# Attention and retention values computed token by token in a hybrid block: whole 512-column products, with the last 16 tokens on their own

## The chip, the cores and the metric

The kernel runs on one core of one Trainium2 chip. The metric is the device time of one execution in microseconds. A core has TensorE (PE, whose weight loads are shown as PEld), VectorE (DVE), ScalarE (ACT), GpSimd (POOL) and the DMA queues of SyncE (SP), ACT and POOL. PE reads its operands from the on-chip memory SBUF and writes to PSUM, eight banks of 512 float32 columns by 128 partitions; DVE and ACT bring results from PSUM back to SBUF.

## The reference

One transformer layer on 512 tokens with 16 meta tokens ahead of them (528 rows, width 1024): a SwiGLU block at half weight, a mixer, a second SwiGLU block, a final norm. The mixer is where the change lies:

```python
proj = u @ w_in                      # u = rmsnorm(h), 528 x 1024
rq, rk, rv, rg, aq, ak, av, iq, ik, iw, g_ret, g_att = split(proj)
# retention: 4 heads, keys of 256, values of 512
y = ((q @ k.T) * decay) @ v          # in chunks, with a carried state
yr = (silu(rg) * rmsnorm(y)) @ w_ret_out
# attention: 8 heads of 128; an index score picks 128 keys for a query
score = sum_h iw_h * relu(iq_h @ ik.T)
ya = softmax(q @ k_selected.T) @ v_selected @ w_att_out
merged = sigmoid(g_ret) * yr + sigmoid(g_att) * ya
h = h + merged @ w_mix_out
```

Both `rv` (4 x 512 columns) and `av` (8 x 128 columns) are products of the same 528 normalized rows with columns of `w_in`.

## The kernel before, in words

Activations lie feature by feature: a tile has 128 features in its partitions and the 528 tokens along its columns. Each float32 operand is split into a high part (an ACT copy rounded to the format fp32r) and a low part (a DVE subtraction of the high part), and a product is three matmuls: high by high, low by high, high by low (`mm3`, L145 to L153, whose matmuls stand at L152). Weights come in by `load_w` (L130, SP's queue) into one of two buffers `raw` of 1 MB, and `split_w` (L136) makes `whi` and `wlo`, three buffers each, by the helper `split` (L116; ACT at L117, DVE at L118). `Cols` (L155) hands out one block of 128 columns after another. The normalization is not applied to the activations themselves: their products are multiplied by R, one over the root mean square of each token, which `rstd_steps` makes (L200).

PE's order is the program's own order, since the kernel schedules PE by hand; on the other engines a scheduler orders instructions by their place in the program and their dependences. While the mixer runs, PSUM has two tiles of two banks (`mm_tile`) and four of one bank (`sm_tile`).

The mixer's stages, in PE's order, are these. First come the index queries (psiq, L573) and the index keys (psik, L588), with rotary tables that POOL multiplies by R (`rope_tables`, L525). Then follow four retention heads (L803 to L877). Each head has two query blocks (psrq), two key blocks (psrk), the output product of the head before (`ret_out`, psro, L701), then four times a gate block (`gated`, psrg, L846) and a value block (`values`, psrv, L854), and once the decayed scores (`decayed`, psst, L745). Steps of a background generator stand between them: index scores (pssc, L606) in head 0, and from head 1's output on the top-k search on DVE (L629).

A value block is 128 value features by 528 tokens, in two halves of 264 columns. The weighted sum needs the tokens in the partitions. So `values` multiplies the block by R on DVE (L857), `by_token` (L788) transposes it on PE in four blocks of 128 tokens and one of 16 (psvt, L791 and L792), and ACT and DVE split the result. The last 16 tokens go into a small stacked tile of 80 rows (`vtail`, by `split_rows`, L654), which is multiplied by an equally stacked tile of scores in one matmul (L775). `weigh` (L777) makes the weighted sum pspv (L774), the squares for the norm, and the gated output.

Attention (L884 to L992) does the same for each of eight heads: query, key and value blocks (psaq, psak, psav; the value at L919), scores (psS, L927), transposed probabilities (psPT, L950), weighted sum (psao, L966), and the transposes of the next value block. Four blocks of the retention's output gates are done behind head 7's scores and the last two after it (L983 to L989, L1000); then come eight gate blocks for attention (psga, L1004), the attention output product (psat), and the mixing product (psmo).

The change replaces `values`, `by_token` and `proj_v` (L919) by one new function, and touches `tails` (L650), `weighted` (L768), `weigh`, `rstd_of` (L210), the index stage (L568 to L603) and both head loops. The first SwiGLU block's last loop (L512 to L519) gets one small POOL instruction per feature block. The second SwiGLU block's output product already has tokens in the stationary operand and 512 features in the moving one (psd, L1146); it is not touched.

Of the kernel before, what the change touches and what calls it, by code (L numbers as in the profile page):

```python
# [18 lines left out]
P = 128  # L19
D = 1024  # L20
# [61 lines left out]
def kernel(ctx: ExitStack, tc: tile.TileContext, x, meta, g1, wg1, wu1, wd1, gm,  # L82
# [117 lines left out]
    def rstd_steps(ssum, n, dim, dst, sp, psum):  # L200


        ends = [min(b * P, n - P) for b in range(-(-n // P))]
        nb = len(ends)
        col = psum()
        for b, t0 in enumerate(ends):
            nc.tensor.matmul(col[:, b : b + 1], ssum[:, t0 : t0 + P], ones, start=True, stop=True)
        yield from rstd_of(col, n, dim, dst, sp, psum, P - (n - S))

    def rstd_of(col, n, dim, dst, sp, psum, tail):  # L210
# [4 lines left out]
        r = sp.tile([P, 5], F32, tag="rcol", name="rcol", bufs=2)  # L215
# [34 lines left out]
    hd = dpool.tile([KD, P, S], F32, name="hd")  # L250

# [4 lines left out]
    gap(cpool, 8)  # L256


    with pool("f1") as fp, pool("gps", 2, PSUM) as gps, ExitStack() as later:
# [205 lines left out]
        for f0, nf in ((0, 12), (12, 10)):  # L465
# [38 lines left out]
            for c in range(0, KD, 2):  # L504
# [61 lines left out]


    with pool("ixt") as ixt:  # L568
# [11 lines left out]
        cos, sin = rope_tables(0, ixt)  # L580
        iq = []
        for i in range(4):
# [4 lines left out]
            iq.append((h, l))  # L587
        w = Cols(w_in, OFF_IK, 1).next()  # L588
# [61 lines left out]
    def tails(p, n):  # L650

        tp.update(v=[stacked(p, f"vtail{i}", P) for i in range(2)], p=stacked(p, "ptail", n), turn=0)
# [27 lines left out]
    with pool("rt") as rt:  # L680
        tp.update(pool=rt, bufs=7)
        cos, sin = rope_tables(2, rt)
        gap(rt, 48)
# [41 lines left out]
        def proj_real(cols, name):  # L725
            w = cols.next()
            ps = sm_tile(name)
            mm3([(ps, REAL)], w, xs, KD)
            return ps

        def proj_all(cols, name):
            w = cols.next()
            parts, ps = halves(mm_tile(name))
            mm3(parts, w, xs, KD)
            return ps

# [31 lines left out]
        def weighted(ps, vb, prob):  # L768

            for kb in range(4):  # L770
                vh, vl = vb[0][:, kb, :], vb[1][:, kb, :]
# [3 lines left out]
            nc.tensor.matmul(ps[:, KQ[4] :], vb[2][:TR], tp["p"][:TR, :NM], start=False, stop=True)  # L775

        def weigh(c, vb, sg, prob, ssum, o):  # L777
# [5 lines left out]
            oh = rt.tile([P, S], F32R, tag=f"oh{c}", name="oh")  # L783
            ol = rt.tile([P, S], F32R, tag=f"ol{c}", name="ol")
            split(t[:, :S], oh, ol)
            o.append((oh, ol))

        def by_token(vt, vp):  # L788
            ps = mm_tile("psvt").rearrange("p (a b) -> p a b", a=2)
            for kb in range(4):  # L790
                nc.tensor.transpose(ps[:, 0, kb * P : (kb + 1) * P], vt[:, kb * P : (kb + 1) * P], ident)  # L791
            nc.tensor.transpose(ps[:NM, 1, 0:P], vt[:, 4 * P : T], ident)  # L792
            vh = vp.tile([P, 4, P], F32R, tag="vh", name="vh", bufs=2)
            vl = vp.tile([P, 4, P], F32R, tag="vl", name="vl", bufs=2)
            split(ps[:, 0, :].rearrange("p (b c) -> p b c", b=4), vh, vl)
            tail = tp["v"][tp["turn"]]
            tp["turn"] ^= 1
            split_rows(ps[:NM, 1, 0:P], tail, "hhl")
            return vh, vl, tail
# [3 lines left out]
        for h in range(RH + 1):  # L803
            if h == RH:
# [4 lines left out]
                break  # L809
            u = rt.tile([P, UW], F32, tag="u", name="u")  # L810
            nc.scalar.dma_start(u, decay[h])
            cols = Cols(w_in, OFF_RQ + h * DK, 2)
            if h == 0:
                steps, bg[0] = bg[0], iter(())
# [9 lines left out]
            cols = Cols(w_in, OFF_RK + h * DK, 2)  # L824
            if h == 0:
                bg[0] = steps
            ka = proj_all(cols, "psrk")
            next(norm, None)
            step()
            kb_ = proj_all(cols, "psrk")  # L830
            next(norm, None)
            rk = rope_pair(ka, kb_, cos, sin, T, "rk")
            step()
# [8 lines left out]
            cv = Cols(w_in, OFF_RV + h * DV, 4)  # L842
# [11 lines left out]
            def values():  # L854
                ps = proj_all(cv, "psrv")
                vt = tmp()
                ins = nc.vector.tensor_tensor(vt, ps, R, ALU.mult)  # L857
                step(ins)
                return vt

            for c in range(4):
                if c == 0:
                    sg = gated()
                    vt = values()
                    prob = decayed(rq, rk, u)
                else:
                    vt = values()
                    sg = gated()
                    weigh(*pend, prob, ssum, o)
# [3 lines left out]
                pend = (c, by_token(vt, rt), sg)  # L873
# [9 lines left out]

    with pool("ao") as ao:  # L884
        ao_parts = []
        with pool("at") as at:
# [11 lines left out]
            cq, ck, cv = (Cols(w_in, o_, AH, step=1) for o_ in (OFF_AQ, OFF_AK, OFF_AV))  # L898
# [20 lines left out]
            def proj_v():  # L919
                w = cv.next()  # L920
                parts, ps = halves(mm_tile("psav"))
                mm3(parts, w, xs, KD)
                vt = tmp()
                nc.vector.tensor_tensor(vt, ps, R, ALU.mult)
                return vt

            def scores(q, k):  # L927
                for j in (3, 2, 1, 0):
# [37 lines left out]
            def weigh_v(parts, v):  # L966
                ps = sm_tile("psao")
                weighted(ps, v, parts)
                oh = ao.tile([P, S], F32R, tag=f"ah{len(ao_parts)}", name="ah")
                ol = ao.tile([P, S], F32R, tag=f"al{len(ao_parts)}", name="al")  # L970
                split(ps, oh, ol)
                ao_parts.append((oh, ol))

            q, k, vt = proj_q(), proj_k(), proj_v()
            for h in range(AH):
                more = h + 1 < AH
                scores(q, k)
                if h == 0:
# [12 lines left out]
                if more:  # L991
                    v = by_token(vt, at)  # L992
# [5 lines left out]
        with pool("ou") as ou:  # L998
            tp.update(pool=ou, bufs=3)
            for c in (6, 7):  # L1000
                gate_acc(c, gate(gr, ou))
            cols = Cols(w_in, OFF_GA, KD)
            sa = []
            for c in range(KD):  # L1004
                w = cols.next()
                ps = sm_tile("psga")
                mm3([(ps, REAL)], w, xs, KD)
                t = ou.tile([P, S], F32, tag=f"sa{c}", name="sa")
                nc.vector.tensor_tensor(t, ps, Rr, ALU.mult)
                nc.scalar.activation(t, t, AF.Sigmoid)  # L1010
                sa.append(t)
# [54 lines left out]
    mgs.close()  # L1066
    accs.close()
# [117 lines left out]
```

## Time and profile before

| | |
|---|---|
| median of 3 runs | 1591.05 us (1590.24 to 1592.95) |
| the profiled execution's own time | 1590.52 us |
| span from its first to its last instruction | 1588.7 us |
| mean granted TensorE clock | 0.999 |
| values in retention / attention (psrv / psav) | 256 / 128 matmuls of each of three kinds |
| value transposes (psvt) | 96 of 128 tokens, 24 of 16 |
| mean memory traffic | 94 GB/s |

In the profile a row of the grouped view gives the source line, the engine, the operation, the output tile and its inputs by the program's names with their shapes, the number of instructions, their busy time and the mean of one in ns, and the idle time of the engine ahead of them with the instruction that ended most of it. Matmuls overlap: the time listed for one is longer than the distance to the next. The chain of waits follows the work back from the last instruction; its pieces are start, length, and what ran. A piece "PE psrv L152 x48" is 48 matmuls in a row without a wait. The table of stages gives, for each stretch, its length, the busy time of PE, PEld, DVE, ACT and POOL, the granted clock, the DMA share and the rate. A wait row gives the line that waited, what it waited for, the total, the number and the longest.

### The profile page before, as it was taken

To read this page: it belongs to the slowest core of one execution; us is meant where nothing else is said; L and a number is where in the kernel's file an instruction comes from. 1 tells how busy PE (TensorE), PEld (TensorE's weight loads), DVE (VectorE), ACT (ScalarE), POOL (GpSimd) and SP (SyncE) were. 2 spreads that over 40 slices of the span, in tenths; PEclk is the share of its full clock that TensorE was granted. 3 is DMA by queue.
4 is the path that set the end of the run, shared out by engine and by line. 5 is a ranking of instruction groups with operands and counts; after the bars stand their busy time and mean duration, and the time that the engine had idled before them with its cause. 6 is when DMAs were issued, how large, how long until landed. Compare 5 with 4: busy or idle time off the path is not lost.

```text
span 1588.7 us, 23011 instructions
## 1 busy us (share of the span) xinstructions
PE 1576.4 (99%) x9731; PEld 1419.7 (89%) x9731; DVE 820.0 (52%) x1263; ACT 569.3 (36%) x912; POOL 230.9 (15%) x187
## 2 busy tenths in 40 slices
PE   9999999999999999999999999999999999999998
PEld 8999999999888898899898999988888888888886
DVE  5443234334575776866845766753454444334434
ACT  6322222223544333233333555552234332223223
POOL 1211001111310201302204110011002111001100
PEclk9999999999999999999999999999999999999999
DMA  5222232224422231231313322322233332232222
GB/s 192 83 89 78 97 109 80 97 80 141 134 88 67 67 116 54 80 117 40 120 54 92 95 67 67 93 72 88 91 128 108 111 105 81 94 113 86 93 92 81
DMA packets 148582, 148.66 MB, mean 94 GB/s; under 512 B 3288, under 2 KB 137456, under 8 KB 148480
## 3 DMA queue, kind: packets, MB, share of 16 engines
q1 hardware_dynamic: 143872, 138.16, 27.0%
q10 hardware_dynamic: 4544, 9.03, 1.7%
q8 instruction: 76, 1.25, 0.3%
q14 instruction: 26, 0.21, 0.0%
q0 software_dynamic: 64, 0.01, 0.0%
HBM read 143.00 MB, written 4.19 MB: 93 GB/s over the span
## 4 chain that ended last, share of the span: by engine, by line
PE 94%; DVE 3%; ACT 1%; issue 1%; POOL 1%; DMA 0%; ACTq 0%; POOLq 0%; DVEq 0%
PE psu L152 16%; PE psg L152 15%; PE psd L152 8%; PE psd L1146 7%; PE psrv L152 6%; PE psrg L152 6%; PE psrk L152 3%; PE psak L152 3%; PE psav L152 3%; PE psrq L152 3%; PE psgate L152 3%; PE psro L152 3%; PE psmo L152 3%; PE psaq L152 3%; PE psat L152 3%; PE psga L152 3%
## 5 line engine op out<-in xcount | busy, mean ns | idle before, releaser
L117 ACT ACTIVATE whi<-raw 128x1024 fp32r<-128x1024 f32 (+3 forms) x284 | 278.0, 981 | 840.1 <-PE psu L152 165.5
L118 DVE TENSOR_TENSOR wlo<-raw,whi 128x1024 fp32r<-128x1024 f32 (+3 forms) x284 | 339.7, 1196 | 177.2 <-ACT whi L117 173.6
L152 PE MATMUL psu<-xl,whi 128*128 128x264 f32 (+1 forms) x528 | 141.0, 319 | 0.0
L152 PE MATMUL psu<-xh,whi 128*128 128x264 f32 (+1 forms) x528 | 140.6, 318 | 0.0
L152 PE MATMUL psu<-xh,wlo 128*128 128x264 f32 (+1 forms) x528 | 140.5, 318 | 0.0
L152 PE MATMUL psg<-xl,whi 128*128 128x264 f32 (+1 forms) x496 | 133.3, 321 | 0.0
L152 PE MATMUL psg<-xh,whi 128*128 128x264 f32 (+1 forms) x496 | 132.8, 320 | 0.0
L152 PE MATMUL psg<-xh,wlo 128*128 128x264 f32 (+1 forms) x496 | 132.8, 321 | 0.0
L152 PEld LDWEIGHTS psu<-xh,wlo 128*128 128x128 f32 x528 | 88.1, 188 | 6.8
L152 PEld LDWEIGHTS psu<-xh,whi 128*128 128x128 f32 x528 | 87.8, 188 | 6.9
L152 PEld LDWEIGHTS psu<-xl,whi 128*128 128x128 f32 x528 | 87.5, 188 | 6.9
L152 PEld LDWEIGHTS psg<-xh,wlo 128*128 128x128 f32 x496 | 82.6, 188 | 6.8
L152 PEld LDWEIGHTS psg<-xh,whi 128*128 128x128 f32 x496 | 82.3, 188 | 6.8
L152 PEld LDWEIGHTS psg<-xl,whi 128*128 128x128 f32 x496 | 82.0, 188 | 6.8
L486 POOL TENSOR_TENSOR t<-t,R 128x528 f32<-128x528 f32 x22 | 37.6, 1711 | 262.3 <-ACT t L485 262.3
L1121 POOL TENSOR_TENSOR t<-t,R 128x512 f32<-128x512 f32 x22 | 38.5, 1751 | 251.6 <-ACT t L1120 251.6
L152 PE MATMUL psd<-hl,whi 128*128 128x264 f32 x352 | 71.3, 284 | 0.0
L152 PE MATMUL psd<-hh,wlo 128*128 128x264 f32 x352 | 70.8, 283 | 0.0
L152 PE MATMUL psd<-hh,whi 128*128 128x264 f32 x352 | 70.6, 282 | 0.0
L1146 PE MATMUL psd<-whi,hh 128*128 128x512 f32 x176 | 68.5, 389 | 0.0
L1146 PE MATMUL psd<-wlo,hh 128*128 128x512 f32 x176 | 68.5, 389 | 0.0
L1146 PE MATMUL psd<-whi,hl 128*128 128x512 f32 x176 | 68.5, 389 | 0.0
(316 smaller groups left out, 3543.1 us busy)
## 6 DMA issues: line engine op xcount, KB each, us to landing
raw<-in_w_in_dram SPq DMA_DIRECT2D x34, 1024.0 KB, 4.9
raw<-in_ffn_w_up_dram SPq DMA_DIRECT2D x22, 1024.0 KB, 5.0
raw<-in_ffn_w_gate_dram SPq DMA_DIRECT2D x21, 1024.0 KB, 5.0
raw<-in_w_in_dram SPq DMA_DIRECT2D x25, 512.0 KB, 3.4
raw<-in_ffn_w_down_dram SPq DMA_DIRECT2D x10, 1024.0 KB, 4.8
raw<-in_w_ret_out_dram SPq DMA_DIRECT2D x16, 512.0 KB, 3.4
raw<-in_ffn_w_down_dram SPq DMA_DIRECT2D x8, 768.0 KB, 4.3
raw<-in_ffn_w_down_dram SPq DMA_DIRECT2D x8, 640.0 KB, 3.9
```

The costliest lines, as they stand in the source:

```text
L117: nc.scalar.activation(hi, src, AF.Copy)
L118: eng.tensor_tensor(lo, src, hi.bitcast(F32), ALU.subtract)
L152: nc.tensor.matmul(o, a[:, k, :], b[:, sl], start=first and k == 0 and i == 0, stop=last and k == nk - 1 and i == 2)
L486: nc.gpsimd.tensor_tensor(t, t, R, ALU.mult)
L1121: nc.gpsimd.tensor_tensor(t, t, R, ALU.mult)
L1146: nc.tensor.matmul(pss[b], a[:, bs], m[:, k % 2, :], start=k0 + k == 0 and i == 0, stop=k0 + k == nf - 1 and i == 2)
```

## The change

`values` is new. It makes four value blocks at once, with 128 tokens as the stationary operand and 512 value features as the moving one, for the 512 tokens of the first four token blocks; two `mm_tile`s hold the four results. A visit goes through the 1024 input features in four quarters of two blocks; in each quarter it takes token blocks 0 to 3 in turn, six matmuls each. In the last quarter the results are split two token blocks at a time, straight from PSUM, with the scale 1/rms of the token as a per-partition scalar (`rtok`, kept by `rstd_of`). After the second quarter stands the product for the last 16 tokens (psvl). Its stationary operand is `xlast`: 32 columns, the last 16 tokens and 16 zeros, in plain float32, made on POOL ahead of time and multiplied by R there. Its moving operand is 128 columns of the unsplit weights in `raw`. The four 128-wide value blocks c = 0 to 3 go to the output partitions 32c to 32c + 31 of one bank, 32 matmuls in all. The result is split, stored to DRAM (`vd`) by two DMAs on POOL's queue, and read back into the stacked tile by three.

There are four visits in retention, one per head, ahead of its scores and gates, and two in attention, of four heads each: one ahead of head 0's scores and one in head 3. The key blocks of retention head 0 are made in the index stage, between the index queries and the index keys, and its rotary tables are made there as well; index scores begin behind its first query block. In attention, gate blocks stand in the heads where value blocks stood (six for the retention gates, then three for the attention gates behind head 7's scores), their weights come one block per load, the weighted sum goes to a two-bank tile, and head 4 takes its widest score tile last.

```diff
+    rtok = cpool.tile([P, 8], F32, name="rtok")
+    xlast = cpool.tile([P, KD, 32], F32, name="xlast")
+    nc.gpsimd.memset(xlast, 0.0)
...
                         h, l = new_x(k, XO)
+                        nc.gpsimd.tensor_scalar(xlast[:, k, :NM], hT[k][:, S:], gains[:, 1, k : k + 1], None, ALU.mult)
                         split_gain(hT[k], gains[:, 1, k : k + 1], h, l)
...
-        norm = rstd_steps(ssum2, T, D, R2, ixt, lambda: mm_tile("psn"))
+        norm = rstd_steps(ssum2, T, D, R2, ixt, lambda: mm_tile("psn"), rtok)
...
+        nc.gpsimd.tensor_tensor(xlast[:, :, :NM], xlast[:, :, :NM], R[:, S:].unsqueeze(1).to_broadcast([P, KD, NM]), ALU.mult)
         cos, sin = rope_tables(0, ixt)
+        ret_tables = rope_tables(2, rtab)
...
+        cols = Cols(w_in, OFF_RK, 2)
+        first_keys = [proj_all(cols, "psrk") for _ in range(2)]
         w = Cols(w_in, OFF_IK, 1).next()
         ps = sm_tile("psik")
...
+    def values(c0, parts, vp, meanwhile=lambda: None):
+        two = [mm_tile("psv") for _ in range(2)]
+        ps = [two[b // 2][:, b % 2 * S : (b % 2 + 1) * S] for b in range(4)]
+        rest = sm_tile("psvl")[:, :P]
+        raws = []
+        for k0 in range(0, KD, 2):
+            if k0 % 4 == 0:
+                raws.append(wpool.tile([P, 2048], F32, tag="raw", name="raw", bufs=2).rearrange("p (k c) -> p k c", k=4))
+            raw = raws[-1]
+            rows = slice(k0 * P, (k0 + 2) * P)
+            nc.sync.dma_start(raw[:, k0 % 4 : k0 % 4 + 2], w_in[rows, c0 : c0 + 4 * P].rearrange("(k p) c -> p k c", p=P))
+        for k0 in range(0, KD, 2):
+            raw = raws[k0 // 4]
+            w_at[0] = XO
+            wh, wl = split_w(raw[:, k0 % 4 : k0 % 4 + 2, :])
+            w_at[0] = 0
+            for b in range(4):
+                bs = slice(b * P, (b + 1) * P)
+                for k in range(2):
+                    xh, xl = xs(k0 + k)
+                    for i, (a, m) in enumerate(((xh, wh), (xl, wh), (xh, wl))):
+                        nc.tensor.matmul(ps[b], a[:, bs], m[:, k, :], start=k0 + k == 0 and i == 0,
+                                         stop=k0 + k == KD - 1 and i == 2)
+                if b % 2:
+                    if k0 == KD - 2:
+                        for d in (b - 1, b):
+                            ds = slice(d * P, (d + 1) * P)
+                            split_gain(ps[d].rearrange("p (c d) -> p c d", c=4), rtok[:, d : d + 1],
+                                       parts[0][:, :, ds], parts[1][:, :, ds])
+                    meanwhile()
+            if k0 == 2:
+                for k in range(KD):
+                    for c in range(4):
+                        nc.tensor.matmul(rest[32 * c : 32 * c + 32], xlast[:, k, :],
+                                         raws[k // 4][:, k % 4, c * P : (c + 1) * P], start=k == 0, stop=k == KD - 1)
+                rh, rl = (vp.tile([P, P], F32R, tag=f"rest{i}", name="rest") for i in range(2))
+                split(rest, rh, rl)
+                for i, part in enumerate((rh, rl)):
+                    nc.gpsimd.dma_start(vd[i], part.bitcast(F32))
+                for r, i in ((0, 0), (32, 0), (64, 1)):
+                    nc.gpsimd.dma_start(tp["v"][r : r + NM].bitcast(F32).rearrange("q (c d) -> q c d", c=4),
+                                        vd[i].rearrange("(c q) d -> q c d", q=32)[:NM])
+        return [(parts[0][:, c, :], parts[1][:, c, :], tp["v"][:TR, c * P : (c + 1) * P]) for c in range(4)]
...
+            vs = values(OFF_RV + h * DV, parts, rt, step)
+            prob = decayed(rq, rk, u)
...
             for c in range(4):
-                if c == 0:
-                    sg = gated()
-                    vt = values()
-                    prob = decayed(rq, rk, u)
-                else:
-                    vt = values()
-                    sg = gated()
+                sg = gated()
+                if c:
                     weigh(*pend, prob, ssum, o)
...
-                pend = (c, by_token(vt, rt), sg)
+                pend = (c, vs[c], sg)
...
+            k, q = proj_k(), proj_q()
+            vs = half_values(0)
             for h in range(AH):
                 more = h + 1 < AH
-                scores(q, k)
-                if h == 0:
-                    v = by_token(vt, at)
+                scores(q, k, *(((2, 1, 0, 3),) if h == 4 else ()))
                 if more:
                     q, k = proj_q(), proj_k()
                 else:
-                    for c in (2, 3, 4):
-                        gate_acc(c, gate(gr, at, wide=True))
-                parts = transpose_p()
-                if more:
-                    vt = proj_v()
+                    wide_gate_a()
+                    wide_gate_a()
+                pt = transpose_p()
+                if h == 3:
+                    more_vs = half_values(1)
+                elif more:
+                    wide_gate()
                 else:
-                    gate_acc(5, gate(gr, at, wide=True))
-                weigh_v(parts, v)
-                if more:
-                    v = by_token(vt, at)
+                    wide_gate_a()
+                weigh_v(h, pt, vs[h])
+                if h == 3:
+                    vs += more_vs
```

More of the change, by code (lines that the diff above doesn't have):

```diff
@@ L681 @@
         tp.update(pool=rt, bufs=7)
-        cos, sin = rope_tables(2, rt)
-        gap(rt, 48)
+        parts = [rt.tile([P, 4, S], F32R, tag=f"vo{i}", name="vo") for i in range(2)]
+        cos, sin = ret_tables
+        gap(rt, 16)
         tails(rt, 64)
@@ L770, in weighted @@
             for kb in range(4):
-                vh, vl = vb[0][:, kb, :], vb[1][:, kb, :]
+                vh, vl = (part[:, kb * P : (kb + 1) * P] for part in vb[:2])
                 ph, pl = prob[kb]
@@ L774, in weighted @@
                     nc.tensor.matmul(ps[:, KQ[kb] :], a, b, start=kb == 0 and i == 0, stop=False)
-            nc.tensor.matmul(ps[:, KQ[4] :], vb[2][:TR], tp["p"][:TR, :NM], start=False, stop=True)
+            nc.tensor.matmul(ps[:, KQ[4] :], vb[2], tp["p"][:TR, :NM], start=False, stop=True)
         def weigh(c, vb, sg, prob, ssum, o):
@@ L782, in weigh @@
             nc.vector.tensor_tensor(t[:, :S], ps, sg, ALU.mult)
-            oh = rt.tile([P, S], F32R, tag=f"oh{c}", name="oh")
-            ol = rt.tile([P, S], F32R, tag=f"ol{c}", name="ol")
+            oh, ol = (part[:, c, :] for part in parts)
             split(t[:, :S], oh, ol)
             o.append((oh, ol))
[L788 to L799, printed above, removed]
         bg = [index_steps()]
@@ L809, with keys @@
                 break
+            def keys():
+                cols = Cols(w_in, OFF_RK + h * DK, 2)
+                ka = proj_all(cols, "psrk")
+                next(norm, None)
+                step()
+                kb_ = proj_all(cols, "psrk")
+                next(norm, None)
+                return ka, kb_
             u = rt.tile([P, UW], F32, tag="u", name="u")
             nc.scalar.dma_start(u, decay[h])
+            if h == 0:
+                rk = rope_pair(*first_keys, cos, sin, T, "rk")
             cols = Cols(w_in, OFF_RQ + h * DK, 2)
-            if h == 0:
-                steps, bg[0] = bg[0], iter(())
             qa = proj_real(cols, "psrq")
@@ L823 @@
             step()
[L824 to L833, printed above, removed]
+            if h:
+                rk = rope_pair(*keys(), cos, sin, T, "rk")
+                step()
             if last_out:
@@ L881, with gate_a @@
             gate_acc(c, t)
+    rtabs.close()
+    sas = ExitStack()
+    sap = sas.enter_context(pool("sap", 1, side="right"))
+    gr = Cols(w_in, OFF_GR + 2 * P, KD - 2, step=1)
+    ga = Cols(w_in, OFF_GA, KD, step=1)
+    sa = []
+    def gate_a(ps, gp):
+        mm3([(ps, REAL)], ga.next(), xs, KD)
+        t = gp.tile([P, S], F32, tag=f"sa{len(sa)}", name="sa")
+        nc.vector.tensor_tensor(t, ps, Rr, ALU.mult)
+        nc.scalar.activation(t, t, AF.Sigmoid)
+        sa.append(t)
     with pool("ao") as ao:
-        ao_parts = []
+        vo = [ao.tile([P, AH, S], F32R, tag=f"vo{i}", name="vo") for i in range(2)]
+        ao_parts = [(vo[0][:, c, :], vo[1][:, c, :]) for c in range(AH)]
         with pool("at") as at:
@@ L917, in proj_k, with half_values, scores @@
                 return k
[L919 to L928, printed above, removed]
+            def half_values(i):
+                return values(OFF_AV + i * 4 * P, [v[:, 4 * i : 4 * i + 4, :] for v in vo], at)
+            def scores(q, k, order=(3, 2, 1, 0)):
+                for j in order:
                     n = NM + P * (j + 1)
@@ L999 @@
             tp.update(pool=ou, bufs=3)
[L1000 to L1011, printed above, removed]
+            while len(sa) < KD:
+                gate_a(sm_tile("psga"), ou)
             cols = Cols(w_ao, 0, KD)
@@ L1066 @@
     mgs.close()
+    sas.close()
     accs.close()
```

60 lines of the change are left out of this document (28 added, 32 removed).

## The prediction

> **What bounds the kernel now.** I read the page first: engine shares, then the chain that ended last.
>
> ```profile
> span 1588.7 us, 23011 instructions
> PE 1576.4 (99%) x9731; PEld 1419.7 (89%) x9731; DVE 820.0 (52%) x1263; ACT 569.3 (36%) x912; POOL 230.9 (15%) x187
> PE 94%; DVE 3%; ACT 1%; issue 1%; POOL 1%; DMA 0%; ACTq 0%; POOLq 0%; DVEq 0%
> ```
>
> PE is busy for 99% of the span and makes 94% of the chain, so a change pays by PE time removed, less the waits it makes. The table of who waited for whom, for PE alone, is short:
>
> ```profile
> PE psg L321 <- DVE idle L289: 1.5, 1, 1.5
> PE psik L152 <- DVE tmp L552: 1.2, 1, 1.2
> PE psrg L152 <- DVE wlo L118: 0.9, 2, 0.6
> PE psst L754 <- DVE tmp L758: 0.5, 1, 0.5
> PE psrq L152 <- ACT tmp L623: 0.5, 1, 0.5
> ```
>
> The first is start-up. The other four (1.2 + 0.9 + 0.5 + 0.5 = 3.1 us) are all the waiting in the part that changes. "Busy" hides how long a matmul really occupies PE (its listed duration overlaps the next one), so I take prices from the chain in order of time, first in retention, then in attention, then the one place that already has the new form:
>
> ```profile
> 577.53 5.78 PE psrv L152 x48
> 583.31 5.48 PE psrg L152 x24
> 588.79 1.96 PE pspv L774 x12
> 590.76 0.50 PE psvt L791 x4
> 591.37 5.77 PE psrv L152 x48
> ...
> 900.84 5.78 PE psav L152 x48
> 906.62 1.96 PE psao L774 x12
> 908.60 0.50 PE psvt L791 x4
> 909.20 2.01 PE psS L939 x15
> ...
> 1353.19 65.28 PE psd L1146 x288
> ```
>
> One 128-wide value block takes 5.77 us (48 matmuls of 264 columns), then its transposes 0.61 us (590.76 to 591.37). A token-stationary matmul with 512 moving columns costs 65.28/288 = 0.2267 us.
>
> **The change part by part.** *Values.* How many there are:
>
> ```profile
> L152 PE MATMUL psrv<-xh,whi 128*128 128x264 f32 x256 | 52.6, 287 | 0.0
> L152 PE MATMUL psav<-xh,whi 128*128 128x264 f32 x128 | 26.3, 287 | 0.0
> L791 PE MATMUL psvt<-ident,tmp 128*128 128x128 f32 x96 | 15.5, 284 | 0.0
> L792 PE MATMUL psvt<-ident,tmp 128*16 128x128 f32 x24 | 6.5, 273 | 0.0
> ```
>
> 256 + 128 are 24 blocks of 16 such matmuls, each block with its transposes. Removed: 24 x 5.77 = 138.5 us and 24 x 0.61 = 14.6 us, 153.1 in all. Added: six visits of 96 matmuls, 576 x 0.2267 = 130.6 us. Difference **-22.5 us**. I trust this most: same form, same widths as L1146.
>
> *The last 16 tokens.* Each visit adds 32 plain float32 matmuls, 128 rows by 32 stationary columns, 128 moving, in four column groups whose outputs lie in different partitions. The trace has no such instruction, so I bound it by its neighbours:
>
> ```profile
> L207 PE MATMUL psn<-ones,ossum 128*128 128x1 f32 x32 | 3.8, 239 | 0.0
> ...
> 462.15 0.17 PE L754 MATMUL psst<-rqh,rkh 128*16 128x16 f32 x1
> ...
> 462.20 0.17 PE L754 MATMUL psst<-rqh,rkl 128*16 128x16 f32 x1
> ...
> 451.14 0.39 PE L152 MATMUL psrg<-xh,wlo 128*128 128x512 f32 x1
> 451.46 0.50 PE L620 MATMUL pssc<-ikh,iqh 64*128 64x512 f32 x2
> 451.80 0.40 PE L620 MATMUL pssc<-ikl,iqh 64*128 64x512 f32 x2
> 452.03 0.39 PE L620 MATMUL pssc<-ikh,iql 64*128 64x512 f32 x2
> 452.36 0.51 PE L152 MATMUL psrv<-xh,whi 128*128 128x264 f32 x2
> 452.70 0.40 PE L152 MATMUL psrv<-xl,whi 128*128 128x264 f32 x2
> ```
>
> L207 issues 4 float32 matmuls per head, 16 in all, and the trace has 32 records: a plain float32 matmul is two passes, so a visit is 64 passes. Nearest row for one pass of 128 float32 moving columns: psvt, 0.50/4 = 0.125 us. Lower bound: the 16-column psst matmuls issue, each with its own weights, three in 0.05 us from first to last, so 0.025 us apart: 64 x 0.025 = 1.6 us. Upper bound: nothing overlaps, 64 x 0.125 = 8.0 us. Which end applies is shown by nothing exactly, but L620 is near: its pairs sit in two row groups, and the second and third pair start 0.23 us apart, one 512-column matmul's time for two. Groups of rows run side by side; I take it that groups of columns do: 16 rounds x 0.125 = 2.0 us. Changing the grouping costs something too: from 451.14 to 452.70 are 1.56 us, and the matmuls explain 0.227 + 3 x 0.23 + 0.24, which leaves 0.40. So 2.0 + 0.4 = 2.4 us a visit (1.6 to 8.4), six visits **+14.4 us**.
>
> The Trainium skill's "TensorE: Matmul & The Clock Gate" (Measured speedup vs the span model) gives 2.38x for three column tiles; scaled to four, 64 x 0.125/3.2 = 2.5 us a visit, an estimate from that page, and the sum would be 3 us higher. Its "TensorEngine Tiling (Array Packing)" (Key Properties) says that changing the mode drains the engine, and the 0.40 us agrees.
>
> *Weights, ACT and DVE.* Splitting a block's weights is the same work (four splits of 1024 columns in place of four). Gone are vt, vl and three small tail steps per block; one split per 128 tokens takes the place of vl. Both engines are at 36 and 52%, so I count nothing; their cover is PE itself.
>
> *Loads.* A visit holds both weight buffers until the float32 matmuls have read them, half-way. Four DMAs bring its weights:
>
> ```profile
> raw<-in_w_in_dram SPq DMA_DIRECT2D x25, 512.0 KB, 3.4
> ```
>
> Both buffers come free when the columns before are split, two or three column groups of PE ahead (2.72 us each in the retention output, over 5 us elsewhere), and the second half is wanted only 10.9 us into the visit. The gate weights behind can start at half-way, 48 x 0.2267 = 10.9 us and the scores' 4 us before use. Zero, and about 2 us a visit if that cover were gone. The tightest DVE stage stays the retention output with top-k:
>
> ```profile
> 645.00:670.00 25.00, 24.38 (x106) 19.36 (x105) 24.66 (x39) 6.31 (x10) 11.46 (x9) 1.00 0.33 106
> 868.00:1087.00 219.00, 218.95 (x1484) 203.70 (x1483) 142.34 (x318) 115.56 (x230) 36.75 (x33) 1.00 0.28 83
> ```
>
> DVE is full there (24.66 of 25). The first values' split now stands where psrg's stood, so the 0.9 us of psrg becomes psv's, not nothing. Eight top-k steps then fall into a visit instead of four into the value blocks; a visit has 21.8 us and needs some 16 us of DVE.
>
> *First head's keys ahead.* Two key blocks move, with their load and splits, in front of the index keys on PE and SP; the tables of head 0 go before the index rope on POOL and ACT's queue. The psik wait (1.2 us) should go: it waited for a PSUM buffer of psiq, and keys use other buffers. But index scores now begin one query block after psik, not after two and a key block:
>
> ```profile
> 416.54 5.68 PE psik L152 x24
> 422.23 10.91 PE psrq L152 x48
> ...
> 432.27 1.38 DVE L603 TENSOR_TENSOR ikl<-tmp,ikh 64x512 fp32r<-64x512 f32 x2 [0.76 <-ACT ikh L602]
> ```
>
> There psik ended at 422.2 and ikl at 433.65, 11.4 us later, much of it queueing behind the rope of iq, which the moved keys now cover. Half of 10.91, 5.5 us, is the new cover. Wait between 0 and 6 us; I take 1.
>
> *Token 512 to 527's inputs.* Eight POOL products of 16 columns stand ahead of the sums of squares at the end of the first FFN, and one of 128 columns ahead of the rope tables:
>
> ```profile
> 398.88 1.82 POOL L245 TENSOR_TENSOR ssum<-ssum,sq 128x528 f32<-128x528 f32 x1 [1.84 <-ACT sq L244]
> ```
>
> POOL idles 1.84 us ahead of the last sum, waiting for ACT: room for a 16-column product, so nothing; without it some 0.2 us.
>
> *Attention.* Gates spread over the heads keep PE work equal. Sigmoid beside Exp makes table loads of 1.28 us, twice a head:
>
> ```profile
> 886.16 1.28 ACT L945 ACT_TABLE_LOAD   x1
> ```
>
> ACT is busy 115.56 of 219 us there and the softmax has a query and a key block (11.2 us) of cover: nothing. After head 3, the widest score tile of head 4 waits for psao's buffer; evacuation is 0.60 (ACT) + 0.69 (DVE), against 1.25 us of narrower scores, with DVE busy: 0.7 us.
>
> *Tail through DRAM.* POOL queues two stores and three loads per visit; behind them stand only sums and rope products of later blocks. The nearest row:
>
> ```profile
> grow<-in_mix_norm_dram POOLq DMA_DIRECT2D x1, 4.0 KB, 4.8
> ```
>
> Two landings are 9.6 us, beginning about 1.5 us after half-visit (10.9 us before its end). In retention the first user comes some 17 us after the visit; in attention head 3's psao comes 2 us after it, so 0 to 3 us once: 1 us.
>
> **Sum.** New waits 0.9 + 1 + 0.7 + 1 = 3.6 us for 3.1 before: +0.5. -22.5 + 14.4 + 0.5 = **-7.6 us** against the profiled execution's own 1590.52 us (span 1588.7 and 1.8 around it): 1582.9, say 1583.0. The runs' median is 1591.05, 0.5 above that execution, which I neglect.
>
> **Rivals.**
> 1. *Column groups run one after another.* Each visit then is 8.0 + 0.4 = 8.4 us: 50.4 - 22.5 + 0.5 = +28.4 us, 1618.9. It decides from (22.5 - 0.5)/6 = 3.7 us a visit. For it: psvt's four follow each other 0.125 us apart, the pairs of L620 differ in rows, and all four column groups use all 128 rows. Against: L620 itself. The Trainium skill's "TensorE: Matmul & The Clock Gate" (The mechanism) says that a weight load overlaps a running matmul only when the row group differs; by that rule this rival holds, but the trace speaks against the rule (PEld is busy for 1419.7 us beside a PE busy for 1576.4). Chance 0.17.
> 2. *Groups run two at a time*, as in L620's pairs: 32 x 0.125 + 0.4 = 4.4 us, 26.4 - 22.5 + 0.5 = +4.4, 1594.9. Chance 0.10.
> 3. *New waits eat the gain*: index scores 6 us, DRAM tail 3 us in place of my 1 and 1 make +7: 1590.0. The 11.4 us speak for it, the shorter queues against. Chance 0.10.
> 4. *Only the move of the keys fails*, psik's place being taken by another PSUM wait: 1.2 us, inside the forecast.
>
> **How the numbers follow.** Forecast 0.63, rivals 0.17, 0.10, 0.10. The forecast's own range: visits of 1.6 us and no waits left give -22.5 + 9.6 - 3.1 = -16.0, 1574.5; visits of 3.2 us (the grouping paid three times, 2.0 + 3 x 0.4) give 1587.7. For 8 in 10 I leave out rival 1 and go from 1574.5 to 1596, which holds rivals 2 and 3. A measurement of this kernel tells 0.2% (3.2 us) from no change. Faster: the forecast nearly whole and half of rival 3, 0.67; same 0.08; slower: rival 1 and most of rival 2, 0.25.
>
> **What would show it.** In the changed profile: psv at 0.227 us a matmul and no psvt; psvl visits 2.4 us long between two psv stretches (8 us: rival 1; 4.4: rival 2); no PE wait on psik, and small ones at pssc, psS and psao. Wrong would be: psv slower than 0.2267, a PE wait on raw or whi at a visit's start, or waits above 7 us in sum.

## The result, and the profile after

The changed kernel takes 1584.12 us (median of 5 runs, 1583.95 to 1584.65); the kernel before, beside it, 1591.05 (1590.24 to 1592.95). The ratio is 0.9955 with a 95% interval of 0.9941 to 0.997: 6.9 us less, against a forecast of -7.6 from the profiled execution and 1583.0 us. The profiled run of the changed kernel took 1584.65 us. Page of the changed kernel:

```profile
span 1582.8 us, 22506 instructions
PE 1570.6 (99%) x9419; PEld 1387.6 (88%) x9419; DVE 800.4 (51%) x1221; ACT 573.8 (36%) x882; POOL 254.3 (16%) x225
PE 96%; DVE 2%; ACT 1%; issue 0%; POOL 0%; ACTq 0%; POOLq 0%
```

PE is still the bound (99% of the span, now 96% of the chain), and it is PE's own time that fell: 1576.4 to 1570.6. The chain in order of time (start, length, what), first over the values of the second retention head, then in the attention:

```profile
561.52 10.89 PE psv L705 x48
572.41 1.89 PE psvl L717 x64
574.29 11.10 PE psv L705 x48
585.40 4.08 PE psst L818 x30
...
919.27 1.96 PE psao L838 x12
921.24 2.10 PE psS L990 x15
```

The transposes are gone and nothing stands between the values and the scores (psst). 48 psv matmuls take 10.89 us, 0.2269 each. The float32 visit takes 1.89 us, and the 48 matmuls behind it 11.10, 0.21 more than those ahead. psS, now right behind psao, takes 2.10 instead of 2.01. Waits of PE (total, times, longest, us):

```profile
PE psg L328 <- DVE idle L296: 1.5, 1, 1.5
PE psrg L152 <- ACT tmp L651: 0.7, 2, 0.4
PE psS L990 <- DVE vo L118: 0.6, 1, 0.6
PE psv L705 <- DVE wlo L118: 0.6, 1, 0.6
PE psrq L152 <- ACT tmp L651: 0.5, 1, 0.5
PE psS L990 <- DVE vo L122: 0.4, 1, 0.4
PE psao L838 <- DVE vo L122: 0.4, 1, 0.4
```

The wait before psik is gone; psS and psao, which did not wait in the kernel before, wait for the values' evacuation (vo). The 0.7 at psrg, in the first head behind the index scores' evacuation (tmp), is new as well. One loss stands in no row: in the first head the three pairs of index scores (pssc), which start at 439.37 us, take 1.45 us up to the next group instead of the 0.89 that they take elsewhere.

One caution for comparing spans: the first psiq matmul starts at 396.5 us in the profile before and at 397.7 in the one after. In the profiles of the experiments below it starts between 396.6 and 397.8, also where the work up to there is the same. So about 1 us of start-up is scatter between profiles, and below "from psiq on" means the span less that start: 1192.2 us before, 1185.1 after, 7.1 less.

### The profile page after: what moved, and what is told of

It is laid out like the page before. It is cut to its first block, busy times and chain, and to the rows that moved or that the text cites. A ratio compares the mean times of both kernels' runs of the same rounds, so it can differ in the third digit from the quotient of the medians.

```text
span 1582.8 us, 22506 instructions
## 1 busy us (share of the span) xinstructions
PE 1570.6 (99%) x9419; PEld 1387.6 (88%) x9419; DVE 800.4 (51%) x1221; ACT 573.8 (36%) x882; POOL 254.3 (16%) x225
## 3 DMA queue, kind: packets, MB, share of 16 engines
q0 software_dynamic: 1024, 1.39, 0.3%
## 4 chain that ended last, share of the span: by engine, by line
PE 96%; DVE 2%; ACT 1%; issue 0%; POOL 0%; ACTq 0%; POOLq 0%
PE psu L152 16%; PE psg L152 15%; PE psv L705 8%; PE psd L152 8%; PE psd L1192 7%; PE psrg L152 6%; PE psro L152 4%; PE psrk L152 3%; PE psak L152 3%; PE psgate L152 3%; PE psmo L152 3%; PE psaq L152 3%; PE psga L152 3%; PE psat L152 3%; PE psrq L152 2%; PE pspv L838 2%
## 5 line engine op out<-in xcount | busy, mean ns | idle before, releaser
L118 DVE TENSOR_TENSOR wlo<-raw,whi 128x1024 fp32r<-128x1024 f32 (+3 forms) x284 | 334.0, 1178 | 207.7 <-ACT whi L117 204.2
L152 PE MATMUL psu<-xh,wlo 128*128 128x264 f32 (+1 forms) x528 | 140.5, 318 | 0.0
L152 PE MATMUL psro<-vo,whi 128*128 128x512 f32 x256 | 79.1, 390 | 0.0
L705 PE MATMUL psv<-whi,xh 128*128 128x512 f32 x192 | 76.0, 396 | 0.0
L705 PE MATMUL psv<-wlo,xh 128*128 128x512 f32 x192 | 74.9, 390 | 0.6 <-DVE wlo L118 0.6
L705 PE MATMUL psv<-whi,xl 128*128 128x512 f32 x192 | 74.8, 390 | 0.0
```

Source lines behind the costliest of these rows:

```text
L118: eng.tensor_tensor(lo, src, hi.bitcast(F32), ALU.subtract)
L152: nc.tensor.matmul(o, a[:, k, :], b[:, sl], start=first and k == 0 and i == 0, stop=last and k == nk - 1 and i == 2)
L705: nc.tensor.matmul(ps[b], a[:, bs], m[:, k, :], start=k0 + k == 0 and i == 0, stop=k0 + k == KD - 1 and i == 2)
```

## The experiments

The first four ask what the float32 visit is made of; each of these kernels, and e_no_narrow below, ran once. **Theory:** the four column groups run side by side. **Rival:** a pass with 32 stationary columns is cheap by itself.

**e_one_group.** All four blocks in the same 32 rows of the output, one block after another (the split and the stores behind follow the new layout):

```diff
-                for k in range(KD):
-                    for c in range(4):
-                        nc.tensor.matmul(rest[32 * c : 32 * c + 32], xlast[:, k, :],
+                for c in range(4):
+                    for k in range(KD):
+                        nc.tensor.matmul(rest[:32, c * P : (c + 1) * P], xlast[:, k, :],
```

> The changed kernel, with the visit's 64 float32 passes all in one column group: the four blocks of features go one after another into the same 32 rows of the output, 128 columns each. Nothing is left out. Theory A, the four column groups of the changed kernel run side by side (1.89 us from first to last pass): without them each pass stands alone, 64 x 0.125 = 8.0 us or more a visit, so 6 x 6.1 = +37 us or more, about 1621. Rival B, a pass with 32 stationary columns is cheap by itself and the groups gain nothing: the visit stays at 1.9 us and the time at 1584.

1615.01 us. Its visit, as start and length of the group of matmuls, and the start of what comes behind:

```profile
576.74 7.17 PE L717 MATMUL psvl<-raw,xlast 128*32 128x128 f32 x64
583.85 0.50 PE L705 MATMUL psv<-whi,xh 128*128 128x512 f32 x1
```

7.11 us from start to start, 0.111 a pass. The same two rows of the changed kernel:

```profile
572.34 1.95 PE L717 MATMUL psvl<-raw,xlast 128*32 128x128 f32 x64
574.22 0.50 PE L705 MATMUL psv<-whi,xh 128*128 128x512 f32 x1
```

1.88 us for the same 64 passes: 3.8 times as fast. From psiq on this kernel takes 31.2 us more, and 6 x (7.11 - 1.88) = 31.4. The theory holds, the rival falls; the forecast's 0.125 us a pass was a little high. A third reading, that passes of one group are slow because they add into the same place of PSUM, was not run. The kernel before speaks against it: its psvt passes write different columns, and by their start times in the trace the second to fourth of a group follow each other 0.109 us apart, as the passes do here.

**e_group_order.** Four groups, but `for c` outside `for k`, so that neighbouring passes share a group.

> The changed kernel with the same four column groups, but all 16 passes of one group before those of the next, so that neighbouring passes share a column group. Nothing is left out. Theory A (groups overlap only where neighbouring passes lie in different groups): the overlap is lost but for three borders, 61 x 0.125 = 7.6 us a visit, about +34 us, 1618. Rival B (the passes are cheap by themselves): 1.9 us a visit and 1584.

1608.43 us. The visit is 5.89 us long:

```profile
576.21 5.96 PE L717 MATMUL psvl<-raw,xlast 128*32 128x128 f32 x64
582.10 0.50 PE L705 MATMUL psv<-whi,xh 128*128 128x512 f32 x1
```

So the overlap needs neighbours in different groups, as the theory says, but 1.22 us of it survive, nearly four passes' worth at each of the three borders instead of one. The stretches of this visit, with the passes in each (the second figure in brackets is of weight loads), show where:

```profile
576.30:577.30 1.00, 1.00 (x10) 1.00 (x11) 0.00 (x0) 0.00 (x0) 1.00 0.00 0
577.30:578.30 1.00, 1.00 (x15) 1.00 (x14) 0.00 (x0) 0.00 (x0) 1.00 0.00 0
```

The first lies inside one group (10 passes running in 1 us), the second over the first border (15). The start times say more: within a group passes are 0.109 us apart, but at each border eight start within 0.36 us. The records do not name the group, so it is inferred, not seen, that the first four passes of the next group begin while the last four of the group before are still to start.

**e_half_width.** 64 moving columns a pass, `c * P : c * P + 64`; half of the last 16 tokens' value features are left out (the other half stands in their place).

> The changed kernel with 64 moving columns instead of 128 in each pass of the visit; leaves out half of the value features of the last 16 tokens (the other half stands in their place). If the 1.89 us are four streams of 128 columns side by side (16 rounds x 0.118), they halve: about 0.95 to 1.0 us a visit, -0.9 x 6 = -5.4 us, 1579.2. If they are 64 issues of 0.0295 us each, the visit stays at 1.9 us and the time at 1584.

1578.85 us, -5.3 (from psiq on -4.9). The visit:

```profile
570.68 1.10 PE L717 MATMUL psvl<-raw,xlast 128*32 128x64 f32 x64
571.71 0.50 PE L705 MATMUL psv<-whi,xh 128*128 128x512 f32 x1
```

1.03 us: half the columns save 0.85. If the time goes with the columns, 128 columns cost 16 x 0.106 = 1.70 us, and 0.18 are fixed. The visit is bound by streaming, not by issue.

**e_no_tail.** Without the visit and its five DMAs; the last 16 tokens' values are left out.

> The changed kernel without the visit and its transfers; leaves out the value part of the last 16 tokens. Price of the visits as a whole. By the trace of the changed kernel 1.89 us of passes and 0.21 us longer for the 48 psv matmuls behind them, 2.1 x 6 = 12.6 us less: span 1570.2, time about 1572.0. The forecast's 2.4 a visit would give 14.4 less, 1570.2. If the weights held through the visit or the transfers on POOL cost something that no row shows, the gain is more than that.

1571.11 us, -13.0 (from psiq on: 1172.4, -12.7). That is 2.1 us a visit; loads held through it and the DMAs on POOL cost nothing beside it.

The next ones ask about the smaller edits.

**e_keys_back.** The changed kernel with the first head's keys behind its queries again, and the index scores held until the queries are done:

```diff
-        cols = Cols(w_in, OFF_RK, 2)
-        first_keys = [proj_all(cols, "psrk") for _ in range(2)]
...
-            if h:
-                rk = rope_pair(*keys(), cos, sin, T, "rk")
-                step()
+            if h == 0:
+                bg[0] = steps
+            rk = rope_pair(*keys(), cos, sin, T, "rk")
+            step()
```

> The changed kernel with the first head's keys back behind its queries, and the index scores held until then, as in the kernel before. Nothing is left out. Forecast: the move takes away the 1.2 us for which TensorE waited before psik, and pays for it with waits in the first head: in the trace of the changed kernel pssc 0.5, psrg 0.7 (the kernel before has 0.9 at psrg in another head and 0.5 at psrq too). So this kernel has the 1.2 at psik again and loses up to 1.2 elsewhere: within 1 us of 1584.1. Rival: the move is worth the whole wait, 1585.3; or more (several us), if the early keys also help the loads.

1586.92 us (1586.57 to 1587.95), 2.8 more than with the move (from psiq on 3.3), where I expected 1 at most. PE's waits in it:

```profile
PE psik L152 <- DVE tmp L560: 3.0, 1, 3.0
...
PE psrq L152 <- DVE wlo L118: 0.6, 1, 0.6
```

The wait before psik is 3.0 us, not the 1.2 of the kernel before, and psrq in the first head waits 0.6 for its weights. What ScalarE and POOL do ahead of it (start, length, engine, line):

```profile
413.79 1.06 ACT L117 ACTIVATE whi<-raw 128x1024 fp32r<-128x1024 f32 x1 [4.52 <-DMA raw<-in_w_in_dram]
414.88 0.61 ACT L234 ACTIVATE R<-psn 128x528 f32<-128x528 f32 x1
...
415.63 0.79 POOL L603 TENSOR_TENSOR xlast<-xlast,R 128x128 f32<-128x128 f32 x1 [11.91 <-ACT R L234]
416.39 1.29 POOL L538 TENSOR_TENSOR cos<-cos,R 128x528 f32<-128x528 f32 x1
```

And in the kernel before:

```profile
412.30 1.06 ACT L117 ACTIVATE whi<-raw 128x1024 fp32r<-128x1024 f32 x1 [4.17 <-DMA raw<-in_w_in_dram]
413.39 0.61 ACT L232 ACTIVATE R<-psn 128x528 f32<-128x528 f32 x1
...
414.08 1.72 POOL L530 TENSOR_TENSOR cos<-cos,R 128x528 f32<-128x528 f32 x1 [10.59 <-DMA raw<-in_w_in_dram]
```

Counted from psiq's start (396.6 and 396.5), R comes 1.4 us later, because the weights that ScalarE splits ahead of it land later; then POOL scales the last tokens' inputs (0.8 us) ahead of cos. cos begins 19.8 us after psiq's start instead of 17.6, and psik waits for a step that needs cos. That the weights land later beside the two tables which the change loads early is argued: from 400 to 416 us the DMA moves 3.20 MB in this kernel, 2.67 in the one before. The early keys hide all of it.

**e_tables_back.** e_keys_back with these POOL products and tables behind the index keys in the program:

```diff
-        nc.gpsimd.tensor_tensor(xlast[:, :, :NM], ...)
...
-        ret_tables = rope_tables(2, rtab)
-        gap(rtab, 32)
...
             nc.vector.tensor_tensor(ikl[r : r + 64], ...)
+        nc.gpsimd.tensor_tensor(xlast[:, :, :NM], ...)
+        ret_tables = rope_tables(2, rtab)
+        gap(rtab, 32)
```

> The kernel with the keys back behind the queries (1586.9, 3.0 us of wait before psik), and with the retention tables and the scaling of the last tokens on GpSimd behind the index keys instead of ahead of the index queries' rotation. Nothing is left out. Theory: the change itself made the wait before psik longer (1.2 in the kernel before): its extra table loads share the DMA with the weights behind which ScalarE makes R (1.4 us later), and the scaling of the last tokens (0.8 us) stands ahead of the tables on GpSimd; the early keys then hide all 3.0. Moved behind, the wait is near 1.2 again and the time near 1585.1. Rival: the longer wait has another cause (the order of PSUM tiles): 3.0 stay, 1586.9.

```profile
PE psik L152 <- DVE tmp L560: 1.9, 1, 1.9
```

The wait fell by 1.1 of the 1.8. The time does not show it: 1587.44 us (1586.30 to 1588.35), within the spread of e_keys_back, though the profiles, from psiq on, differ by 0.6 (1187.9 against 1188.5). The scheduler still issued the table loads early, ahead of the weights' landing at 413.3:

```profile
406.55 0.33 ACTq L536 DMA_DIRECT2D cos<-in_rope_dram  x1
```

Counted from psiq's start, cos begins at 18.3 us instead of 19.8. Of these 1.5 us, 0.8 are the scaling of the last tokens, which now stands behind cos on POOL, and 0.7 are R, which comes earlier with the weights ahead of it (17.6 instead of 18.3). So POOL's part of the longer wait is shown in the trace. R is still 0.7 later than in the kernel before, and whether the table loads cause that stays open.

**e_keys_only.** The kernel before with the key move alone.

> The kernel before with the key move alone (the first head's keys projected ahead of the index keys, their tables loaded with the index tables). Nothing is left out. Forecast: -1.2 for the wait before psik, +1 (0 to 6) for the index scores that then wait for the index keys: 1590.8, same as before within 0.2%. Rival: -1.2 and no new wait, 1589.9, or a wait of several us, 1595.

1593.19 us (1592.42 to 1594.88) against 1591.65 of the kernel before beside it: 1.5 us slower, ratio 1.0011 (1.0002 to 1.002). The wait before psik is gone, but

```profile
PE psst L760 <- DVE tmp L764: 2.0, 3, 1.0
```

was 0.5 before. One of the three waits (1.0 us at 463.1) lies in the first head, where the index scores now come earlier; that they keep VectorE from the decayed scores there is argued. The other two (0.8 at 685.2 and 0.2 at 791.3) lie in the third and fourth heads, where no index scores stand; the kernel before has 0.5 in the third. What makes them longer is open. In the changed kernel psst comes behind all the values (561.52 to 585.40 in the second head, 23.9 us) and does not wait. So the key move pays only with the rest of the change: alone it costs 1.5 us, and taking it out of the change costs 2.8.

**e_per_block.** Each token block read out right behind its last matmul, instead of two together:

```diff
+                if k0 == KD - 2:
+                    split_gain(ps[b]..., rtok[:, b : b + 1], parts[0][:, :, bs], parts[1][:, :, bs])
                 if b % 2:
-                    if k0 == KD - 2:
-                        for d in (b - 1, b):
-                            ...
```

> The changed kernel with each token block of the values read out of PSUM right behind its last matmul, instead of two blocks together. Nothing is left out. Theory: the 1.4 us that TensorE waits in the attention (psS 0.6 and 0.4, psao 0.4) stand at the end of the values, where ScalarE and VectorE have two blocks to read (0.69 + 0.75 us each) before the next PSUM tile is free; if the third block is read 1.36 us earlier, most of it goes: -0.7 to -1.4, 1582.7 to 1583.4, with nothing lost in the retention heads, whose values end without a wait. Rival: VectorE is late anyway for other work at these places, and nothing changes.

1610.07 us (1608.61 to 1614.14): 26 us slower, so my theory failed. PE's waits, and the chain at the end of one visit:

```profile
PE psv L705 <- DVE vo L122: 21.8, 12, 3.0
```

```profile
588.88 3.03 PE psv L705 x12
591.90 0.02 issue
591.93 0.70 ACT vo L121
592.62 0.03 issue
592.65 0.76 DVE vo L122
593.41 0.04 issue
593.46 1.68 PE psv L705 x6
```

Two blocks share one PSUM tile of two banks. Once the first is being read, the six matmuls of the second, which write the other bank, wait until the read is done, twice a visit: 12 waits. Taking two blocks together is what makes this layout run; I had costed it at nothing.

**e_steps_late.** The index scores held until the first head's queries are done (`steps, bg[0] = bg[0], iter(())` ahead of them, `bg[0] = steps` behind).

> The changed kernel with the index scores held until the first head's queries are done (the keys stay early). Nothing is left out. Theory: the waits at pssc 0.5, psrq 0.5 and psrg 0.7 in the first head come from index scores that start too early and take VectorE and ScalarE there; held back, the scores spread over more of TensorE's work and 0.5 to 1.2 us go: 1582.9 to 1583.6. Rival: the same work on ScalarE and VectorE only moves behind the values, and TensorE waits there instead: 1584.1 or up to 2 us more.

1583.72 us (1583.31 to 1584.33): 0.4 less (from psiq on 0.7), and the runs of both kernels overlap. Its chain shows the scores behind the values' first matmuls, with no wait between:

```profile
444.11 2.73 PE psv L705 x12
446.84 0.28 PE psw L637 x3
447.12 0.89 PE pssc L648 x6
```

So the theory holds for pssc alone: its 0.56 us are back, while psrg (0.8) and psrq (0.5) wait as before.

**e_no_narrow.** Without the 16-column matmul that ends each weighing (L839): the last 16 tokens' part of the result is left out.

> The changed kernel without the narrow matmul (16 moving columns) that ends each weighing of the values; leaves out what the last 16 tokens add to the last 16 rows, 24 times. Theory: the next weight load has nothing to lie beside during a matmul of 16 columns, so the group behind starts about 0.10 us late (psrg, psrq and psgate behind it 5.57 us instead of 5.47, psS 2.10 instead of 2.00; the 0.61 us that the forecast took for the transposes held the same 0.10). Without it these groups are back at 5.47 and 2.00: 24 x 0.11 = 2.6 us less, counted from psiq's start. Rival: the 0.10 belongs to the following group itself; it stays, and only the narrow matmul's own 0.01 goes: 0.2 to 0.3 us less.

1581.68 us; from psiq on 1182.9, 2.2 less. The chain's groups behind a weighing, in this kernel and then in the changed one:

```profile
601.70 5.47 PE psrg L152 x24
609.13 5.47 PE psrg L152 x24
```

```profile
602.60 5.57 PE psrg L152 x24
610.14 5.57 PE psrg L152 x24
```

The rival falls: the narrow matmul costs the group behind it 0.10 us. It does so in 20 of the 24 places; in the other four, in the first head, index scores follow and next to nothing comes back, so 2.2 and not 2.6. By the start times, the second psrg matmul follows the first after 0.31 us behind the narrow matmul and after 0.24 without it. That it waits there for its weight load is argued.

**e_score_order.** The widest score tile last in head 0 too, and one bank for head 3's weighing:

```diff
-                scores(q, k, *(((2, 1, 0, 3),) if h == 4 else ()))
+                scores(q, k, *(((2, 1, 0, 3),) if h in (0, 4) else ()))
-                ps = mm_tile("psao")[:, :S]
+                ps = sm_tile("psao") if h == 3 else mm_tile("psao")[:, :S]
```

> The changed kernel with the narrower score tiles ahead of the widest one in attention head 0 too, and the fourth head's weighing in a one-bank PSUM tile. Nothing is left out. Theory: the 1.4 us at psS (0.6 and 0.4) and psao (0.4) are waits for the two-bank tile that the values leave; other work comes first then, and 0.6 to 1.4 us go: 1582.7 to 1583.5. Rival: the wait moves to the next user of a PSUM tile, 1584.1.

1581.99 us (1581.85 to 1582.46), 2.1 less, more than the 1.4 of the listed waits, all three of which are gone. The changed kernel's chain at one of them:

```profile
1003.44 0.69 ACT vo L121
1004.13 0.02 issue
1004.16 0.76 DVE vo L122
1004.92 0.14 issue
1005.06 2.22 PE psao L838 x12
```

Its last psv matmul starts at 1004.23 and psao at 1005.06, 0.83 us later where matmuls follow each other in 0.227: 0.60 are lost, while the waits list 0.4, because they count from a matmul's recorded end (0.39 us).

**e_both.** e_steps_late and e_score_order together.

> The changed kernel with the index scores held until the first head's queries are done (alone 1583.7) and the order of score tiles and the one-bank tile of the run beside this one. Nothing is left out. Theory: the two add, as they lie 400 us apart: 0.4 + 0.6 to 1.4 less, 1582.3 to 1583.1. Rival: nothing beyond the 0.4, 1583.7.

1581.26 us (1581.17 to 1581.89), ratio to the kernel before 0.9937 (0.9924 to 0.995). It beats both kernels: 2.9 us less than the changed one.

## Why the prediction was right, step by step

The sum came out (-7.6 forecast, -6.9 by the medians, -7.1 from psiq on), the likeliest case was the true one, but not every term was.

- **Values, -138.5 + 130.6.** Right: psv takes 0.2269 us a matmul, 576 make 130.7.
- **Transposes, -14.6.** Too much. The 0.61 us from one chain row to the next held 0.10 that the narrow matmul L775 leaves to whatever follows; psvt paid it before, psrg pays it now. 24 x 0.51 = 12.2. The trace of the kernel before agrees: from the start of the first psvt matmul to the start of the next group, the 24 places add up to 12.2 us. That psvt paid these 0.10 is inferred from e_no_narrow; no run takes the narrow matmul out of the kernel before.
- **The visits, +14.4.** 2.4 us each were forecast; they cost 2.1 (1.88, and 0.1 each on the way in and out), 12.7 in all by e_no_tail. The mechanism, four side by side, is shown by e_one_group. The round was mis-sized, 0.106 instead of 0.125. The row it came from, 0.50 us for four psvt, holds a first step of 0.155 us; the other three are 0.109 apart, and so are the rounds of the visit. What is left, 2.09 - 1.70 = 0.39, is as much as the 0.40 taken for the switching, but only 0.2 of it lie at the borders; that the other 0.18, within the visit, are switching is not shown. Rivals 1 and 2 are out. The Trainium skill's "TensorE: Matmul & The Clock Gate" (The mechanism) lists a weight load as overlapping running matmuls only when the row group differs, though the text ahead of that list also allows a background weight buffer. The 3.8 times here, with all groups on all 128 rows, do not agree with the list.
- **Weights and loads, zero; POOL's edits, zero.** Right for weights and loads during the visits (e_no_tail), and for the rest only because of the cover: e_keys_back shows 3.0 us before psik, 1.8 more than before.
- **Keys ahead, -1.2 + 1.** The wait went and the index scores cost 0.6 by the rows (0.4 by the medians of e_steps_late), not 1. But the move is worth 2.8 us in this kernel and -1.5 alone; the forecast treated it as a separate item.
- **Attention, +0.7; DRAM tail, +1; DVE-full stage, 0.9.** The DRAM tail cost nothing: no PE wait on vtail. The attention's PSUM waits cost 2.1 (e_score_order): the forecast saw head 4's widest tile and missed head 0's, and psao's own wait in head 3. In the DVE-full stage psv waits 0.6 for wlo. The forecast had no term for psrg's 0.7 in the first head, which comes with the new order of the values (it is in e_keys_back and not in e_keys_only), nor for psrq's 0.5, which stayed.

So the mechanism and the large terms were right, and that the sum came out within 0.5 us is in part luck: errors of +2.4 (transposes), about +1.4 (attention) and +1.2 (psrg, psrq) stood against -1.7 (visits), -1 (DRAM), -0.4 (index scores) and -0.3 (psv for wlo). These come to +1.6, and the forecast missed by +0.5, so they leave about 1 us open. A second count says the same: what is left for all waits is -7.1 + 7.9 + 12.2 - 12.7 = +0.3 us, while the waits listed (3.2 without start-up, against 3.1), the 0.7 that the list leaves out in the attention and the 0.6 at pssc make +1.4. Counted from each matmul's start to the next one's, the trace holds the whole difference: -140.5 (psrv, psav), -12.2 (psvt), +135.1 (psv), +11.3 (psvl) and -0.7 (all others) are -7.0. So the open 1 us is not outside PE's own order of matmuls; it lies in the steps where one group follows another, which I have not taken apart.

## What to carry to other kernels

Take the price of a removed instruction from the whole stretch with and without it: what it paid for its neighbour stays behind. An edit that costs nothing may owe it to another edit of the same change, so undo each alone before keeping or dropping it. When two blocks share a PSUM tile, read them out together, and let work with another PSUM tile come first behind them.

## What the runs showed that I had not expected

- Column groups of float32 passes run almost fully side by side: 64 passes in 1.88 us against 7.11 in one group.
- With 16 passes of a group in a row, the next group still runs beside the last four or so: 5.89 us instead of 7.11.
- A PSUM tile of two banks was waited for as one: 12 waits, 21.8 us.
